# Decoder trunk on one core: start addresses of matmul operands in SBUF, and the place of the column sums in the half steps

## Chip, core and metric

The kernel runs on one core of one Trainium2 chip. The metric is the device time of one execution in microseconds (us); lower is better. Three runs of the kernel before gave 1283.91, 1286.25 and 1288.17 us. Engines are named as the profile names them: PE is the matmul engine (TensorE), PEld its loads of stationary operands, DVE is VectorE, ACT ScalarE, POOL GpSimd, SP SyncE.

## What is computed

A decoder trunk of two layers on x of 256 rows by 1024 columns, all in float32. Each layer is a half step, a mixer with three attention branches, and a second half step. A half step is the feed-forward block:

```python
D_MODEL, SEQ, DEPTH, D_FF = 1024, 256, 2, 2816

def rms_norm(x, g):
    y = x * lax.rsqrt(jnp.mean(x * x, axis=-1, keepdims=True) + EPS)
    return y * g

def swiglu_ffn(x, g, wi, wo):
    a, b = jnp.split(rms_norm(x, g) @ wi, 2, axis=-1)
    return (jax.nn.silu(a) * b) @ wo

for l in range(DEPTH):
    x = x + 0.5 * swiglu_ffn(x, ffn1_norm[l], ffn1_wi[l], ffn1_wo[l])
    h = rms_norm(x, mix_norm[l])
    ...
    x = x + y @ w_out[l]
    x = x + 0.5 * swiglu_ffn(x, ffn2_norm[l], ffn2_wi[l], ffn2_wo[l])
```

## The kernel before

**Weights.** All weights of a layer lie in HBM as a stream of slabs of 128 rows by up to 1024 columns. SP fetches a slab in pieces of 512 columns into `raw`; ACT rounds a piece to its high half (L524) and DVE subtracts to get the low half (L525). The mixer's own loader does the same in L980 and L982. `next_slab` keeps two slabs ahead of the one in use. A product of two split numbers takes three matmuls: high by high, low by high, high by low.

**Two pools hold split slabs.** `slab_tiles` puts a slab into `whi` and `wlo` (pool `wp`, four buffers each, alive all the time) or, within a half step, into `vhi` and `vlo` (pool `fp`, four buffers each, alive during the half step). In a half step slabs 0 to 3 go to `wp`, and slab 6 too (in the first half step of all, slab 8 in its place); so do the 22 slabs of the last half step's down projection.

**Transposed matmuls.** In a half step and in the output projection of the mixer the slab is the stationary operand (128 columns of it at a time), and the moving operand is the activation, transposed, 256 columns for the two tiles of 128 rows. `chunk_T` (L740 to L742) multiplies `hThi`, `hTlo` with the slabs of the up projections: a first chunk "both" of four slabs, whose accumulators hold one gate and one value block, and then, for each chunk of columns, the slabs of the gate and those of the value. `out_T` (L647 to L649) multiplies the result `gh`, `gl` with the down projection, or, at the end of a mixer, `yT` with the output projection. These are 6192 matmuls of 256 columns. The mixer's other projections are the other way round: the slab moves (up to 512 columns) and `hThi`, `hTlo` are stationary (L577 to L579). In the last half step the down projection is in that form too.

**Row scales.** The norm's row factor is applied behind the product. `out_T` adds up squares of the new x in `sq` (L607, L609, and the last addition L611); `sum_squares` lets PE sum the columns with a vector of ones (L617); DVE and POOL make 1/sqrt from it (L623 to L628); `spread_rn` lets PE turn the factors into rows (L719 to L721). Accumulators that are complete before `rows` exists wait in `pend`, and are evacuated when `spread_rn` runs. A phase has eight steps, two for each slab; `scale_cols` is called behind step 5 and `spread_rn` behind step 3, counted from 0. In the first half step of all, `scale_cols` runs in the first gate phase and `spread_rn` in the first value phase behind it; in the other three half steps both come a phase earlier, in the chunk "both" and in the first gate phase.

**Order.** PE runs in the order of the code (a manual schedule). In the mixer, a `Planner` with a clock for each engine settles the order of PE, DVE and ACT when the program is built. Elsewhere the order on DVE and ACT is settled by the framework's scheduler at build time. Within an engine, work is done strictly in that order.

**Where operands begin.** The pools lay tiles one behind another in each partition, so a tile's size shifts those behind it. In the built program the start addresses, modulo 512 bytes, are:

| operand | role in the transposed matmuls | before | after |
|---|---|---|---|
| `hThi`, `hTlo` | moving | 0 | 192 |
| `gh`, `gl` | moving | 0 | 192 |
| `yT` | moving | 320 | 192 |
| `whi`, `wlo` | stationary | 0 | 0 |
| `vhi` | stationary | 192 | 0 |
| `vlo` | stationary | 448 | 0 |

The 128 columns of a stationary operand are 512 bytes and the 256 columns of a moving one are 1024, so every matmul of a kind has the same remainder. For the mixer's `hThi`, `hTlo` and the last half step's `gh`, `gl`, which are stationary, the remainder is 0 in both kernels.

Of the kernel before, what the change touches and what calls it, by code (L numbers as in the profile page):

```python
# [10 lines left out]
F = mybir.dt.float32  # L11
R = mybir.dt.float32r
# [341 lines left out]
WARM = 9  # L354
TAIL = 3

MIX_SLABS = 69
# [13 lines left out]
def decoder_trunk(ctx, tc, xt_in, wts, lcon, cst, out, depth=DEPTH):  # L371
# [21 lines left out]
    def big_tile(name, dt=F, shape=(128, D)):  # L393
        return hp.tile(list(shape), dt, tag="hy", name=name, bufs=6)
# [102 lines left out]
    def slab_tiles(i):  # L497


        j = stream[i][1] % (len(plan) - FFN_SLABS)  # L500
        end = FFN_SLABS - DFF // 128 if i >= len(stream) - FFN_SLABS else FFN_SLABS
        if not 4 <= j < end or j == 6 and i != j or i == 8:
            return tuple(wp.tile([128, 1024], R, tag=t, name=t) for t in ("whi", "wlo"))
        if own:
            return own.pop()
        return tuple(fpool[0].tile([128, 1024], R, tag=t, name=t, bufs=W_BUFS) for t in ("vhi", "vlo"))
# [79 lines left out]

    def new_T():

        n = NT * D
        return tuple(hp.tile([128, n + p], R, tag=t, name=t)[:, p:].rearrange("p (k t n) -> p k t n", t=NT, n=128)  # L590
                     for t, p in (("hThi", 128), ("hTlo", 0)))

# [44 lines left out]

    def out_T(src, kts, gi, between=None, scale=None):

# [17 lines left out]
        sls = [next_slab() for _ in range(TAIL)]  # L657
        hq, sq = nxt[0] = new_T(), big_tile("sq")
        for b in range(KT // 2):
# [35 lines left out]
    def ffn(l, gi):  # L695
        first = l == 0 and gi == 0
        last = l == depth - 1 and gi == 2
        if first:
            nxt[0] = new_T(), big_tile("sq")
        hq, sq = nxt[0]  # L700
        with ExitStack() as es:
            fp = fpool[0] = es.enter_context(tc.tile_pool(name="fp", bufs=2))
            gq = (fp.tile([128, 96 + DFF * NT], R, name="gh", bufs=1)[:, 96:].rearrange(
                      "p (k t n) -> p k t n", t=NT, n=128),
                  fp.tile([128, DFF * NT + 48], R, name="gl", bufs=1)[:, :DFF * NT].rearrange(
                      "p (k t n) -> p k t n", t=NT, n=128))
            vhi = fp.tile([128, 1024], R, tag="vhi", name="vhi", bufs=W_BUFS)
            rows = fp.tile([128, 320], F, name="rows", bufs=1)[:, 0:S].rearrange("p (t n) -> p t n", t=NT)
            own.append((vhi, fp.tile([128, 1024], R, tag="vlo", name="vlo", bufs=W_BUFS)))
# [3 lines left out]
            def spread_rn():  # L713

                tp = tp_tile()
                b = fp.tile([128, 512], F, tag="gate", name="rnb")
                for t in range(NT):
                    c = slice(t * 128, (t + 1) * 128)
                    nc.vector.tensor_copy(b[:, c], rn[t][:, 0:1].to_broadcast([128, 128]))  # L719
                    nc.tensor.transpose(tp[:, c], b[:, c], ident)  # L720
                nc.scalar.activation(rows.rearrange("p t n -> p (t n)"), tp[:, 0:S], AF.Copy)  # L721
                for f in pend:
                    f()
                del pend[:]
                spread[0] = True

# [19 lines left out]

            spread, gates = [False], {}

            def soon(f, *a):
                if spread[0]:  # L750
                    f(*a)
                else:
                    pend.append(lambda: f(*a))
# [75 lines left out]
            if first:  # L829
                first_steps()  # L830
            else:
                drain(chunk_T(512, both), lambda i: scale_cols() if i == 5 else None)

# [10 lines left out]
            def hook(i):  # L844
                if ci == 0 and first:
                    if i == 5:
                        scale_cols()
                elif ci == 0 and i == 3:
                    spread_rn()
                if last and ci and i == 3:  # L850
                    x_rows(ci - 1)
                hook2(i)

            def first_spread(i):
                if i == 3:
                    spread_rn()
                hook2(i)
# [5 lines left out]
            for ci, (f0, fn) in enumerate(FFN_CHUNKS[1:]):  # L863
# [8 lines left out]
                drain(chunk_T(fn, gate_T), hook)  # L872
                drain(chunk_T(fn, value_at(f0 // 128)), first_spread if first and ci == 0 else hook2)

# [5 lines left out]
            else:  # L880
                def scale(a):
                    u = fp.tile([128, 512], F, tag="g", name="u")
                    by_rows(u, a)
                    return u
                out_T(gq, DFF // 128, 3 * l + gi + 1, between, scale)


    def mixer(l):
# [38 lines left out]
        pl = Planner()  # L927
        spawn = pl.spawn
        ordered = tc.manual_schedule(engines={nc.vector.engine, nc.scalar.engine})
        ordered.__enter__()  # L930
# [111 lines left out]
        def scales():  # L1042

            k = yield "P", 0.4, 0.6, (Tok(7.0),), (s_tp,)
            a = sum_squares(sq)
# [896 lines left out]
        def y_first(t):  # L1942
            k = yield use_t(4, ev_y[0][t], slots=(s_tp,))
            if not yT:
                yT.extend(mp.tile([128, 128 + NT * 1024], R, tag=f"V{i}", name="yT")[:, 80:80 + NT * 1024].rearrange(
                    "p (k t n) -> p k t n", t=NT, n=128) for i in (1, 0))
# [29 lines left out]
        nc.scalar.preload_act_table_set("silu_and_others")  # L1976
        out_T(yT, KT, 3 * l + 2, y_T)
        es.close()
# [40 lines left out]
```

## Time and profile before

| | before |
|---|---|
| median of 3 runs | 1286.25 us |
| profiled execution: its own time | 1286.52 us |
| profiled execution: span from the first to the last instruction | 1284.4 us |
| mean granted TensorE clock | 0.997 |
| DVE busy | 928.2 us (72%) |
| ACT busy | 790.1 us (62%) |
| read from HBM | 254.91 MB, 225 GB/s over the span |

The span is 2.1 us shorter than the time of its execution; times within the kernel below are counted from the span's start. The stages can be told from the first use of their operands on PE: first half step to 192.9 us, mixer to 434.9, its output projection and the second half step to 640.8, first half step of the second layer to 828.9, mixer to 1069.4, and the rest to the end.

Matmuls overlap in their pipeline. The duration of one in the profile (about 280 ns for 256 columns) is longer than the distance from its start to the next one's start, and it is that distance that adds up to the time.

### The profile page before, as it was taken

The page shows a single profiled execution, that of the slowest core. Times are in us where ns is not written, and L with a number is a line of the kernel's source. Part 1 is how long each engine was busy: PE and PEld are TensorE (multiplying, and loading weights), DVE is VectorE, ACT ScalarE, POOL GpSimd, SP SyncE. Part 2 cuts the span into 40 slices and gives each one's busy share as a digit, 9 for nine tenths or more (in the row PEclk, how much of TensorE's full clock was granted, in tenths as well). Part 3 has the DMA queues.
Part 4 walks back from the last instruction along what each step waited for, and adds up shares of the span by engine and source line. Part 5 has one row for each costly group of instructions (what it writes and reads, how often), then busy time and mean ns, then how long its engine had stood idle before and what let it go on. Part 6 is the DMA issues. An engine that isn't in the chain of part 4 may idle for free.

```text
span 1284.4 us, 25746 instructions
## 1 busy us (share of the span) xinstructions
PE 1266.3 (99%) x9215; PEld 1174.9 (91%) x9215; DVE 928.2 (72%) x1924; ACT 790.1 (62%) x1627; POOL 104.7 (8%) x164
## 2 busy tenths in 40 slices
PE   9999999999999999999989999999999999999998
PEld 9999998878877899999989999988888779999987
DVE  7776667978898776776667676779768887765653
ACT  6555557777887465565545565577757774655542
POOL 0012100210000001121000121011100000000000
PEclk9999999999999999999989999999999999999999
DMA  8789985556645567899757899664786455566653
GB/s 282 249 285 330 339 284 175 178 181 212 205 127 169 165 221 240 279 333 332 253 165 266 287 336 349 207 195 149 256 289 218 141 170 166 187 189 183 213 164 115
DMA packets 150959, 291.74 MB, mean 227 GB/s; under 512 B 17840, under 2 KB 19504, under 8 KB 150832
## 3 DMA queue, kind: packets, MB, share of 16 engines
q1 hardware_dynamic: 140976, 258.12, 62.0%
q0 software_dynamic: 9856, 31.99, 6.7%
q8 instruction: 72, 1.18, 0.4%
q14 instruction: 55, 0.45, 0.1%
HBM read 254.91 MB, written 34.60 MB: 225 GB/s over the span
## 4 chain that ended last, share of the span: by engine, by line
PE 85%; DVE 5%; ACT 4%; DMA 2%; issue 2%; POOL 0%; SPq 0%; DVEq 0%; ACTq 0%
PE acc L740 12%; PE acc L742 12%; PE acc L741 12%; PE acc L577 9%; PE acc L579 9%; PE acc L578 9%; PE acc L647 5%; PE acc L648 5%; PE acc L649 5%; DMA raw<-in_wts 2%; PE tp L1545 1%; DVE wlo L982 1%; ACT whi L980 1%; DVE hTlo L599 1%; ACT wf L1504 1%
## 5 line engine op out<-in xcount | busy, mean ns | idle before, releaser
L525 DVE TENSOR_TENSOR vlo<-raw,vhi 128x512 fp32r<-128x512 f32 x444 | 288.0, 687 | 107.0 <-ACT vhi L524 106.4
L524 ACT ACTIVATE vhi<-raw 128x512 fp32r<-128x512 f32 x444 | 258.2, 622 | 156.7 <-PE acc L741 53.5
L740 PE MATMUL acc<-hThi,vhi 128*128 128x256 f32 x1248 | 346.9, 278 | 0.0
L742 PE MATMUL acc<-hThi,vlo 128*128 128x256 f32 x1248 | 346.5, 278 | 0.0
L741 PE MATMUL acc<-hTlo,vhi 128*128 128x256 f32 x1248 | 346.2, 277 | 0.0
L741 PEld LDWEIGHTS acc<-hTlo,vhi 128*128 128x128 f32 x1248 | 234.4, 188 | 0.0
L742 PEld LDWEIGHTS acc<-hThi,vlo 128*128 128x128 f32 x1248 | 234.4, 188 | 0.0
L740 PEld LDWEIGHTS acc<-hThi,vhi 128*128 128x128 f32 x1248 | 234.2, 188 | 0.0
L577 PE MATMUL acc<-whi,hThi 128*128 128x512 f32 (+2 forms) x416 | 163.4, 393 | 0.0
L579 PE MATMUL acc<-whi,hTlo 128*128 128x512 f32 (+2 forms) x416 | 158.6, 381 | 0.0
L578 PE MATMUL acc<-wlo,hThi 128*128 128x512 f32 (+2 forms) x416 | 158.1, 380 | 0.0
L982 DVE TENSOR_TENSOR wlo<-raw,whi 128x512 fp32r<-128x512 f32 x216 | 141.3, 679 | 21.3 <-ACT whi L980 20.1
L980 ACT ACTIVATE whi<-raw 128x512 fp32r<-128x512 f32 x216 | 126.3, 617 | 43.1 <-PE acc L579 23.3
L649 PE MATMUL acc<-gh,vlo 128*128 128x256 f32 x528 | 146.4, 277 | 0.0
L647 PE MATMUL acc<-gh,vhi 128*128 128x256 f32 x528 | 146.3, 277 | 0.0
L648 PE MATMUL acc<-gl,vhi 128*128 128x256 f32 x528 | 146.3, 277 | 0.0
L525 DVE TENSOR_TENSOR wlo<-raw,whi 128x512 fp32r<-128x512 f32 x116 | 75.5, 684 | 44.0 <-ACT whi L524 43.7
L524 ACT ACTIVATE whi<-raw 128x512 fp32r<-128x512 f32 x116 | 68.0, 621 | 58.6 <-PE acc L579 26.4
L544 DVE TENSOR_TENSOR elo<-eraw,ehi 128x512 fp32r<-128x512 f32 x60 | 41.5, 692 | 84.1 <-ACT ehi L543 84.1
L543 ACT ACTIVATE ehi<-eraw 128x512 fp32r<-128x512 f32 x60 | 37.9, 632 | 103.8 <-DMA eraw<-in_wts 100.4
L648 PEld LDWEIGHTS acc<-gl,vhi 128*128 128x128 f32 x528 | 99.2, 188 | 0.0
L649 PEld LDWEIGHTS acc<-gh,vlo 128*128 128x128 f32 x528 | 99.1, 188 | 0.0
(319 smaller groups left out, 2417.4 us busy)
## 6 DMA issues: line engine op xcount, KB each, us to landing
raw<-in_wts SPq DMA_DIRECT2D x764, 256.0 KB, 3.3
eraw<-in_wts SPq DMA_DIRECT2D x60, 256.0 KB, 5.1
early<-ehi POOLq DMA_DIRECT2D x60, 256.0 KB, 4.0
early<-elo POOLq DMA_DIRECT2D x60, 256.0 KB, 4.5
whi<-early SPq DMA_DIRECT2D x60, 256.0 KB, 3.8
wlo<-early SPq DMA_DIRECT2D x60, 256.0 KB, 3.9
xd<-x SPq DMA_DIRECT2D x4, 512.0 KB, 2.7
x<-xd SPq DMA_DIRECT2D x4, 512.0 KB, 3.6
```

The costliest lines, as they stand in the source:

```text
L524: nc.scalar.activation(hi[:, c:c + m], raw[:, :m], AF.Copy)
L525: nc.vector.tensor_tensor(lo[:, c:c + m], raw[:, :m], hi[:, c:c + m], op=OP.subtract)
L577: nc.tensor.matmul(o, a[0], b[0], start=start, stop=False)
L578: nc.tensor.matmul(o, a[0], b[1], start=False, stop=False)
L579: nc.tensor.matmul(o, a[1], b[0], start=False, stop=stop)
L647: nc.tensor.matmul(o, sl[0][:, w], h, start=k == 0 and c == 0, stop=False)
L648: nc.tensor.matmul(o, sl[0][:, w], l_, start=False, stop=False)
L649: nc.tensor.matmul(o, sl[1][:, w], h, start=False, stop=k == kts - 1 and c == 1)
L740: nc.tensor.matmul(o, sl[0][:, w], h, start=k == 0 and c == 0, stop=False)
L741: nc.tensor.matmul(o, sl[0][:, w], l_, start=False, stop=False)
L742: nc.tensor.matmul(o, sl[1][:, w], h, start=False, stop=k == KT - 1 and c == 1)
L982: nc.vector.tensor_tensor(hl[1][:, c:c + m], raw[:, :m], hl[0][:, c:c + m], op=OP.subtract)
```

## The change

All slabs now begin at multiples of 512 bytes, whether in `wp` or in `fp`, and the moving operands of the transposed matmuls begin 192 bytes (`MOVING` = 48 elements) behind such a multiple; `new_T` and `out_T` take that shift as `at`. The exceptions for slabs 6 and 8 go. `scale_cols` and `spread_rn` stand where they stood in the first half step, for all four. In the mixer the planner starts with DVE's clock at 7.0 and ACT's at 3.0, and takes the column sums to be possible at 10.0 in place of 7.0.

```diff
+MOVING = 48
...
-        if not 4 <= j < end or j == 6 and i != j or i == 8:
+        if not 4 <= j < end:
             return tuple(wp.tile([128, 1024], R, tag=t, name=t) for t in ("whi", "wlo"))
...
-    def new_T():
+    def new_T(at):
         n = NT * D
-        return tuple(hp.tile([128, n + p], R, tag=t, name=t)[:, p:].rearrange("p (k t n) -> p k t n", t=NT, n=128)
-                     for t, p in (("hThi", 128), ("hTlo", 0)))
+        return tuple(hp.tile([128, n + 128], R, tag=t, name=t)[:, at:at + n].rearrange("p (k t n) -> p k t n", t=NT, n=128)
+                     for t in ("hThi", "hTlo"))
...
-            nxt[0] = new_T(), big_tile("sq")
+            nxt[0] = new_T(MOVING), big_tile("sq")
...
-            gq = (fp.tile([128, 96 + DFF * NT], R, name="gh", bufs=1)[:, 96:].rearrange(
-                      "p (k t n) -> p k t n", t=NT, n=128),
-                  fp.tile([128, DFF * NT + 48], R, name="gl", bufs=1)[:, :DFF * NT].rearrange(
-                      "p (k t n) -> p k t n", t=NT, n=128))
+            at = 96 if last else MOVING - 32
+            gq = tuple(fp.tile([128, DFF * NT + n], R, name=nm, bufs=1)[:, at:at + DFF * NT].rearrange(
+                "p (k t n) -> p k t n", t=NT, n=128) for nm, n in (("gh", 128), ("gl", 96)))
...
-            rows = fp.tile([128, 320], F, name="rows", bufs=1)[:, 0:S].rearrange("p (t n) -> p t n", t=NT)
+            rows = fp.tile([128, S], F, name="rows", bufs=1).rearrange("p (t n) -> p t n", t=NT)
...
-                drain(chunk_T(512, both), lambda i: scale_cols() if i == 5 else None)
+                drain(chunk_T(512, both))
...
             def hook(i):
-                if ci == 0 and first:
-                    if i == 5:
-                        scale_cols()
-                elif ci == 0 and i == 3:
-                    spread_rn()
+                if ci == 0 and i == 5:
+                    scale_cols()
...
-                drain(chunk_T(fn, value_at(f0 // 128)), first_spread if first and ci == 0 else hook2)
+                drain(chunk_T(fn, value_at(f0 // 128)), spread if ci == 0 else hook2)
...
-                out_T(gq, DFF // 128, 3 * l + gi + 1, between, scale)
+                out_T(gq, DFF // 128, 3 * l + gi + 1, 0 if gi == 0 else MOVING, between, scale)
...
         pl = Planner()
         spawn = pl.spawn
+        pl.clock.update(V=7.0, A=3.0)
...
-            k = yield "P", 0.4, 0.6, (Tok(7.0),), (s_tp,)
+            k = yield "P", 0.4, 0.6, (Tok(10.0),), (s_tp,)
...
-                yT.extend(mp.tile([128, 128 + NT * 1024], R, tag=f"V{i}", name="yT")[:, 80:80 + NT * 1024].rearrange(
+                yT.extend(mp.tile([128, 128 + NT * 1024], R, tag=f"V{i}", name="yT")[:, MOVING:MOVING + NT * 1024].rearrange(
...
-        out_T(yT, KT, 3 * l + 2, y_T)
+        out_T(yT, KT, 3 * l + 2, MOVING, y_T)
```

PE, second half step of the first layer, around the column sums (`att` from `sq`). Before, they stand behind the third slab, `whi_6138`:

```order
L740 MATMUL acc_6137<-hThi_6024,whi_6138 128x256
L741 MATMUL acc_6137<-hTlo_6025,whi_6138 128x256
L742 MATMUL acc_6137<-hThi_6024,wlo_6139 128x256
L617 MATMUL att_6238<-gcol_106,sq_6026 128x1 x2
L740 MATMUL acc_6136<-hThi_6024,whi_6172 128x256
```

Now they stand behind the seventh, `vhi_6274`:

```order
L740 MATMUL acc_6273<-hThi_6024,vhi_6274 128x256
L741 MATMUL acc_6273<-hTlo_6025,vhi_6274 128x256
L742 MATMUL acc_6273<-hThi_6024,vlo_6275 128x256
L618 MATMUL att_6376<-gcol_106,sq_6026 128x1 x2
L740 MATMUL acc_6272<-hThi_6024,vhi_6308 128x256
```

From the half step's start to the sums, PE has 168 matmuls in place of 72, and the same holds in the second layer's two half steps.

DVE at the start of the first mixer, where the squares' last addition (`sq` 128x256) releases the column sums. Before:

```order
L599 SCALAR_TENSOR_TENSOR hTlo_2685<-x_75,gcol_106,hThi_2684 128x256 x2
L609 TENSOR_TENSOR sq_2686<-sq_2686 128x512
L982 TENSOR_TENSOR wlo_2895<-raw_2896,whi_2894 128x512
L611 TENSOR_TENSOR sq_2686<-sq_2686 128x256
L982 TENSOR_TENSOR wlo_2895<-raw_2903,whi_2894 128x512
L623 TENSOR_SCALAR ss_2921<-att_2906 128x2
```

And now:

```order
L600 SCALAR_TENSOR_TENSOR hTlo_2685<-x_75,gcol_106,hThi_2684 128x256 x2
L610 TENSOR_TENSOR sq_2686<-sq_2686 128x512
L980 TENSOR_TENSOR wlo_2898<-raw_2899,whi_2897 128x512
L980 TENSOR_TENSOR wlo_2898<-raw_2906,whi_2897 128x512
L612 TENSOR_TENSOR sq_2686<-sq_2686 128x256
L624 TENSOR_SCALAR ss_2924<-att_2902 128x2
```

The last addition has moved behind one more low half of a slab. On PE the sums stand behind the mixer's first 36 matmuls in both kernels.

DVE in the second half step of the first layer, from the row factors (`rn`) to the first evacuations (`gate`, `g`, `gl`). Before:

```order
L628 TENSOR_SCALAR rn<-rs 128x2 x3
L719 COPY rnb<-rn 128x128 x2
L544 TENSOR_TENSOR elo<-eraw,ehi 128x512
L525 TENSOR_TENSOR vlo<-raw,vhi 128x512 x4
L756 TENSOR_TENSOR gate<-acc,rows 128x512
L769 TENSOR_TENSOR g<-acc,gate 128x512
L756 TENSOR_TENSOR gate<-acc,rows 128x512
```

And now:

```order
L629 TENSOR_SCALAR rn<-rs 128x2 x3
L719 COPY rnb<-rn 128x128 x2
L526 TENSOR_TENSOR vlo<-raw,vhi 128x512 x2
L545 TENSOR_TENSOR elo<-eraw,ehi 128x512
L526 TENSOR_TENSOR vlo<-raw,vhi 128x512 x4
L756 TENSOR_TENSOR gate<-acc,rows 128x512 x2
L769 TENSOR_TENSOR g<-acc,gate 128x512
L526 TENSOR_TENSOR vlo<-raw,vhi 128x512
L756 TENSOR_TENSOR gate<-acc,rows 128x512
```

Four accumulators, not two, now wait for the row factors, and three slabs' low halves, not two, stand between the factors and the first evacuation.

More of the change, by code (lines that the diff above doesn't have):

```diff
@@ L636, in drain, with out_T @@
                 hook(i)
-    def out_T(src, kts, gi, between=None, scale=None):
+    def out_T(src, kts, gi, at, between=None, scale=None):
         accs = [acc_tile() for _ in range(KT // 2)]
@@ L657, in out_T @@
         sls = [next_slab() for _ in range(TAIL)]
-        hq, sq = nxt[0] = new_T(), big_tile("sq")
+        hq, sq = nxt[0] = new_T(at), big_tile("sq")
         for b in range(KT // 2):
@@ L724, in spread_rn @@
                 del pend[:]
-                spread[0] = True
+                spreaded[0] = True
             def chunk_T(n, evac):
@@ L745, in chunk_T @@
                         yield
-            spread, gates = [False], {}
+            spreaded, gates = [False], {}
             def soon(f, *a):
-                if spread[0]:
+                if spreaded[0]:
                     f(*a)
@@ L852, in hook, with spread @@
                 hook2(i)
-            def first_spread(i):
+            def spread(i):
                 if i == 3:
```

## The prediction

> **What bounds the kernel now.** I read the page's head and its chain first, then PE's windows stage by stage, then what PE waited for.
>
> ```profile
> span 1284.4 us, 25746 instructions
> PE 1266.3 (99%) x9215; PEld 1174.9 (91%) x9215; DVE 928.2 (72%) x1924; ACT 790.1 (62%) x1627; POOL 104.7 (8%) x164
> ...
> PE 85%; DVE 5%; ACT 4%; DMA 2%; issue 2%; POOL 0%; SPq 0%; DVEq 0%; ACTq 0%
> ```
>
> PE is busy 99% of the span and carries 85% of the chain that ended last. So a change pays only if it takes away one of PE's few waits, or if a matmul takes less time from its start to the next one's. The second is not in a duration: it is a window's length over the number of matmuls in it.
>
> ```profile
> core 0: us, PE busy (x), PEclk, DMA share, GB/s
> 17.20:25.30 8.10, 8.10 (x74) 1.00 0.79 252
> 25.70:192.80 167.10, 167.10 (x1420) 1.00 0.87 298
> 438.10:458.30 20.20, 20.20 (x174) 1.00 0.50 156
> 471.80:640.80 169.00, 169.00 (x1492) 1.00 0.86 289
> 641.00:649.30 8.30, 8.30 (x71) 1.00 0.12 36
> 654.20:659.60 5.40, 5.40 (x26) 0.50 0.75 278
> 668.40:828.80 160.40, 160.40 (x1418) 1.00 0.86 292
> 1072.60:1092.80 20.20, 20.20 (x174) 1.00 0.48 155
> 1106.30:1133.80 27.50, 27.50 (x243) 1.00 0.54 172
> 1134.20:1220.30 86.10, 86.10 (x735) 1.00 0.64 195
> ```
>
> All are windows of the same matmul, 256 columns of float32, with PE never idle. The count holds the two or three that had begun before the window, so I take 2.4 off. 668.4 to 828.8 gives 160.4 / 1415.6 = 113.3 ns; 25.7 to 192.8 gives 167.1 / 1417.6 = 117.9; 641.0 to 649.3 gives 8.3 / 69 = 120. Three paces, then, at the same granted clock. I call them A (113.3), B (117.8) and C (120.0). The mean duration of a group tells them apart as well:
>
> ```profile
> L740 PE MATMUL acc<-hThi,vhi 128*128 128x256 f32 x296 | 81.7, 276 | 0.0
> L740 PE MATMUL acc<-hThi,vhi 128*128 128x256 f32 x257 | 71.7, 279 | 0.0
> L740 PE MATMUL acc<-hThi,whi x24: 283/283/283, 640.8 to 649.1; 128*128 128x256 f32 x24
> L647 PE MATMUL acc<-yT,whi x48: 279/279/363, 441.3 to 458.0; 128*128 128x256 f32 x48
> ```
>
> 276 ns is A (480 to 640 us), 279 B (40 to 180), 283 C. C belongs to `whi`, the one stationary operand that begins, modulo 512 bytes, where its moving operand does. A and B share their addresses (`hThi` at 0, `vhi` at 192, `vlo` at 448), so between these two it isn't the address alone. What turns A into B is a break in the stream:
>
> ```profile
> 25.02 0.28 PE L740 MATMUL acc<-hThi,vhi 128*128 128x256 f32 x1
> ...
> 25.36 0.50 PE L617 MATMUL att<-gcol,sq 128*128 128x1 f32 x4
> 25.72 0.36 PE L740 MATMUL acc<-hThi,vhi 128*128 128x256 f32 x1
> ...
> 26.16 0.28 PE L740 MATMUL acc<-hThi,vhi 128*128 128x256 f32 x1
> ...
> 26.52 0.28 PE L740 MATMUL acc<-hThi,vhi 128*128 128x256 f32 x1
> ```
>
> Three matmuls take 0.34 us before the column sums (25.02 to 25.36) and 0.36 behind them, and it stays so for 167 us. Between the last two windows above stand the transposes of `x_rows` at 1133.8 us, and the pace changes there too (27.5 us for 243, 86.1 for 735). The way back to A leads, wherever the trace shows it, through a slab in `whi` at pace C:
>
> ```profile
> L740 PE MATMUL acc<-hThi,vhi 128*128 128x256 f32 x8 | 2.2, 279 | 0.0
> L740 PE MATMUL acc<-hThi,whi 128*128 128x256 f32 x7 | 2.0, 283 | 0.0
> L740 PE MATMUL acc<-hThi,vhi 128*128 128x256 f32 x7 | 1.9, 276 | 0.0
> ```
>
> These are three windows one behind another, 662.6 to 665.1, 665.8 to 668.2 and 668.7 to 671.0 us: B before slab 6, C in it, A behind it, until 828.8.
>
> **The change part by part.** The profiled execution took 1286.52 us, 0.3 above the median, so what I take off it is taken off the median too.
>
> *Column sums a phase later.*
>
> ```profile
> 649.33 0.28 PE L742 MATMUL acc<-hThi,wlo 128*128 128x256 f32 x1
> 653.29 0.99 PE L617 MATMUL att<-gcol,sq 128*128 128x1 f32 x4 [3.68 <-DVE sq L611]
> ...
> PE att L617 <- DVE sq L611: 8.9, 5, 3.7
> PE att L617 <- DVE sq L611: 1.1, 1, 1.1
> PE att L617 <- DVE sq L611: 1.7, 1, 1.7
> ```
>
> PE waits five times for DVE's last addition of squares, 8.9 us in all; the last two rows are the two mixers' (windows at 190 and 830 us). The three half steps hold 8.9 - 1.1 - 1.7 = 6.1 us. In the largest, `sq` is ready for PE at 653.3, 12.5 us behind the first matmul at 640.8. With 168 matmuls ahead of them the sums come 168 x 0.1133 = 19.0 us behind it: 6.5 us of room, so the wait goes. With it goes the half clock behind it (0.50 from 654.2 to 659.6): 5.4 us for some 25 matmuls that take 25 x 0.1133 = 2.8, and the sums' own 0.85 us (653.29 to 654.14) against 0.36 in the first half step, 0.5. Together 6.1 + 2.6 + 0.5 = 9.2 us.
>
> What is late next? The first half step already runs the new order: its window from 25.7 to 192.8 is busy for 167.10 of 167.10 us, with `spread_rn` and four held accumulators in it. The other three add two `ehi`/`elo` pieces in that stretch. DVE works off three low halves of two pieces (0.68 us each, by the row of the next part) and one `elo` before the first evacuation, 7 x 0.68 = 4.8 us if none is done ahead, and PE needs the next accumulator 48 matmuls or 5.4 us behind the row factors' transposes. That is cover of 0.6 us; I take nothing, and 1 us for each of three at worst.
>
> *Mixer.* There the sums keep their place on PE, and the last addition moves behind one more low half:
>
> ```profile
> 200.12 0.68 DVE L982 TENSOR_TENSOR wlo<-raw,whi 128x512 fp32r<-128x512 f32 x1
> 200.72 0.42 DVE L611 TENSOR_TENSOR sq<-sq 128x256 f32<-128x256 f32 x1
> ```
>
> PE waits for it already, so each mixer loses the 0.60 us from start to start: +1.2. The planner's other moves swap groups of matmuls without adding any; the two waits there, 1.1 + 1.7 us, bound them either way: -2.8 (both gone) to +2.8.
>
> *Addresses.* No matmul is added. B fills 167.1 + 20.2 + 20.2 + 86.1 = 293.6 us of the windows above. At A they would take 113.3 / 117.8 of that: -11.2. C is run by the 480 matmuls with `whi` against `hThi`, less some 80 at other paces: 400 x 6.7 ns = 2.7. So if everything ran at A, -13.9. If everything ran at B, A's windows (8.1 + 169.0 + 160.4 + 27.5 = 365 us) grow by 117.8 / 113.3: +14.5, and C's 400 save 2.2 ns each: -0.9. If everything ran at C: 365 x 0.0591 + 293.6 x 0.0187 = +27.1. Moving at 192 against stationary at 0 occurs nowhere in the trace; `yT` at 320 against 0 is the nearest row, and it ran at B (279 ns) from breaks on. I still take A. After a break, a distance of zero ends at C and one of 192 or 448 at B, so the distance does choose the pace; and every distance seen, counted stationary less moving, is 0 or 192 modulo 256 (192, 448, and 0 - 320), while the new one, 0 - 192, is 64. It is a new case, and A is the pace at which half of the matmuls with a distance other than zero already run. With no distance of zero left, what made C goes too.
>
> The Trainium skill's page "SBUF — State Buffer", section "Who interferes with whom", gives TensorE separate read ports for the moving operand and for the weight load and says that it never waits on anyone. By that rule start addresses do nothing; here 276 and 283 ns for `vhi` and `whi` speak against it.
>
> The sum: 1286.5 - 9.2 + 1.2 - 13.9 = 1264.6, so **1265 us**. Its own range is 1261 (the mixers' waits gone and their 1.2 too) to 1270 (planner +2.8, held accumulators +3).
>
> **The rivals.** (1) *Every break ends in B, and nothing leads back.* For it: `yT`, `vhi` behind 25.36 and `vhi` behind 1133.8. The change takes out the `whi` slab that led back to A, and each half step has two breaks or more. Then 1286.5 - 9.2 + 1.2 + 14.5 - 0.9 = 1292, slower. It decides as soon as B holds over about 60% of what is A now, since only 9.2 - 1.2 + 0.9 = 8.9 us stand against 14.5. Against it: the distance is one not seen. (2) *Addresses do nothing in sum*, whether because A and B are spread by chance as now or because they don't matter at all: 1286.5 - 9.2 + 1.2 = 1278.5, perhaps 1.5 less for C. For it: the same addresses gave A and B. This is also what the skill's rule gives. (3) *A new wait takes the place of the old one*: the four held accumulators stop PE at the second chunk of columns. The three later half steps then wait some 2 us each, and with paces as now the time is 1278.5 + 6 = 1284.5, no change. Against it: the first half step. (4) *The new distance is as bad as zero*: C everywhere, 1286.5 - 8.0 + 27.1 = 1306.
>
> **How the numbers follow.** A everywhere 0.55; (2) 0.22; (1) 0.15; (3) 0.04; (4) 0.04. A difference of 0.3%, 3.9 us, is about what a measurement of this kernel can tell from none. A and nearly all of (2) are faster, 0.76; (3) and the edge of (2) and (1) are no change, 0.07; the rest of (1), and (4), are slower, 0.17. A alone holds too little, and with (2) it is 0.77 at most, so the range reaches to (1): 1260 to 1294.
>
> **What would show it.** `L740` to `L742` and `L647` to `L649` at 276 ns in all stages, `yT` too: A. 279 in long stretches: (1) or (2), by where they lie. 283: (4). PE's wait for `sq` gone in the half steps, some 4 us left in the mixers, and a clock of 1.00 at 650 us: the first term. A wait of PE on DVE `gate` or `g` some 33 us into a half step: (3). I am wrong if a distance of -192 is no different from one of 192 or 320.

## Result and profile after

| | median | lowest to highest | runs |
|---|---|---|---|
| before, same chip | 1286.07 us | 1283.91 to 1288.17 | 4 |
| after | 1276.88 us | 1273.79 to 1277.69 | 4 |

The ratio is 0.9924, with a 95% interval of 0.9901 to 0.9947: 9.2 us faster, where 21 were forecast. The time lies within the predicted range; the gain is less than half of the predicted one. The profiled execution after took 1273.79 us, the fastest of the four, so the profile shows a gain of 12.7 us, not of 9.2. The readings from profiles below explain the 12.7.

The head and the chain of the page after:

```profile
span 1271.7 us, 25740 instructions
PE 1257.2 (99%) x9215; PEld 1166.3 (92%) x9215; DVE 925.7 (73%) x1923; ACT 788.5 (62%) x1628; POOL 108.0 (8%) x164
...
PE 90%; DVE 4%; ACT 3%; DMA 2%; issue 1%; POOL 0%; ACTq 0%; DVEq 0%
```

PE still bounds it, with 90% of the chain in place of 85%. PE's windows after, all in the 256-column matmuls, except for the last two, which lie in the mixers just behind the column sums (columns: window, its length, PE busy and number of matmuls, granted clock with 1.00 for PE's full clock, DMA share, GB/s):

```profile
25.70:34.00 8.30, 8.30 (x73) 1.00 0.97 332
34.50:186.00 151.50, 151.50 (x1338) 1.00 0.89 307
479.00:640.00 161.00, 161.00 (x1421) 1.00 0.84 285
649.00:658.00 9.00, 9.00 (x81) 1.00 0.75 254
658.60:808.00 149.40, 149.40 (x1319) 1.00 0.86 297
1126.00:1146.00 20.00, 20.00 (x173) 1.00 0.62 178
1148.00:1170.00 22.00, 22.00 (x196) 1.00 0.59 193
197.70:201.00 3.30, 3.30 (x10) 0.53 0.27 90
826.60:831.60 5.00, 5.00 (x15) 0.50 0.36 114
```

Taking 2.4 off each count as before: the three long windows give 113.4 to 113.5 ns, pace A, the first of them where the kernel before ran 117.9. Pace B is left behind the column sums (8.3 / 70.6 = 117.6, some 72 matmuls until the row factors' transposes) and behind two of the four breaks by `x_rows` (20.0 / 170.6 = 117.2; the next stretch, 22.0 / 193.6 = 113.6, is A again). At 650 us the clock is 1.00 now. But the last two rows show what wasn't there before: the clock halves in the mixers.

What PE waited for, and the two column sums of the mixers (start, duration, engine, line, what; in brackets how long PE idled and for whom):

```profile
PE att L618 <- DVE sq L612: 4.4, 2, 2.3
PE tp L1663 <- DMA zc<-wf: 2.5, 2, 1.7
```

```profile
197.01 0.67 PE L618 MATMUL att<-gcol,sq 128*128 128x1 f32 x4 [2.28 <-DVE sq L612]
825.62 0.98 PE L618 MATMUL att<-gcol,sq 128*128 128x1 f32 x4 [2.13 <-DVE sq L612]
```

The half steps' waits for `sq` are gone. The mixers' have grown from 1.06 and 1.69 us to 2.28 and 2.13. The same before: the row of the waits, the two sums, and the clock behind the second:

```profile
PE tp L1665 <- DMA zc<-wf: 1.3, 1, 1.3
```

```profile
201.29 0.58 PE L617 MATMUL att<-gcol,sq 128*128 128x1 f32 x4 [1.06 <-DVE sq L611]
837.90 0.58 PE L617 MATMUL att<-gcol,sq 128*128 128x1 f32 x4 [1.69 <-DVE sq L611]
```

```profile
838.60:843.20 4.60, 4.60 (x23) 1.00 0.53 161
```

Before, 23 matmuls lie in 4.6 us at full clock; after, 15 of the same kind in 5.0 us at half.

**Stage by stage.** Each length is the distance from the first matmul of a stage to the first of the next, in the profiled execution of each kernel, in us. The half steps 2 and 4 are counted with the output projection ahead of them. e1 to e12 are the experiments below.

| kernel | half step 1 | mixer 1 | half step 2 | half step 3 | mixer 2 | half step 4 |
|---|---|---|---|---|---|---|
| before | 187.8 | 242.0 | 206.0 | 188.0 | 240.5 | 215.0 |
| after | 181.9 | 244.9 | 203.4 | 180.5 | 244.4 | 211.2 |
| e1 after again | 181.6 | 248.7 | 203.4 | 187.5 | 240.7 | 211.2 |
| e2 mixer sums later | 181.3 | 240.6 | 203.4 | 180.5 | 238.8 | 211.1 |
| e3 addresses only | 182.3 | 246.9 | 205.3 | 194.2 | 240.1 | 215.4 |
| e4 order only | 187.8 | 246.8 | 204.4 | 187.0 | 241.6 | 213.6 |
| e5 mixer as before | 181.4 | 242.3 | 203.4 | 180.9 | 244.3 | 211.1 |
| e6 moving at 320 | 188.6 | 240.3 | 209.3 | 187.2 | 238.1 | 214.4 |
| e7 moving at 256 | 191.2 | 243.0 | 214.6 | 190.7 | 238.7 | 217.1 |
| e8 best | 182.5 | 239.1 | 203.4 | 180.9 | 237.9 | 209.5 |
| e9 moving at 448 | 182.0 | 238.8 | 203.4 | 180.6 | 237.8 | 209.9 |
| e10 moving at 128 | 189.3 | 238.7 | 212.4 | 188.6 | 237.9 | 215.5 |
| e11 best again | 181.5 | 238.7 | 203.4 | 180.5 | 237.9 | 209.5 |
| e12 other order of `x_rows` | 184.2 | 239.6 | 203.4 | 180.6 | 237.9 | 209.5 |

From before to after the half steps give 5.9 + 2.6 + 7.5 + 3.9 = 19.9 us, where 23.1 were forecast, and the mixers take 2.9 + 3.9 = 6.8 back, where 1.2 were forecast; 0.4 more lies ahead of the first stage. That is the 12.7.

### The profile page after: what moved, and what is told of

It is laid out like the page before. It is cut to its first block, busy times and chain, and to the rows that moved or that the text cites. A ratio compares the mean times of both kernels' runs of the same rounds, so it can differ in the third digit from the quotient of the medians.

```text
span 1271.7 us, 25740 instructions
## 1 busy us (share of the span) xinstructions
PE 1257.2 (99%) x9215; PEld 1166.3 (92%) x9215; DVE 925.7 (73%) x1923; ACT 788.5 (62%) x1628; POOL 108.0 (8%) x164
## 4 chain that ended last, share of the span: by engine, by line
PE 90%; DVE 4%; ACT 3%; DMA 2%; issue 1%; POOL 0%; ACTq 0%; DVEq 0%
PE acc L740 12%; PE acc L741 12%; PE acc L742 12%; PE acc L578 10%; PE acc L580 10%; PE acc L579 10%; PE acc L648 5%; PE acc L649 5%; PE acc L650 5%; DMA raw<-in_wts 1%; PE tp L1543 1%; DVE wlo L980 1%; ACT whi L978 1%; PE att L1895 1%; DMA zc<-wf 1%
## 5 line engine op out<-in xcount | busy, mean ns | idle before, releaser
L740 PE MATMUL acc<-hThi,vhi 128*128 128x256 f32 x1280 | 355.6, 278 | 0.0
L742 PE MATMUL acc<-hThi,vlo 128*128 128x256 f32 x1280 | 354.7, 277 | 0.0
L741 PE MATMUL acc<-hTlo,vhi 128*128 128x256 f32 x1280 | 354.6, 277 | 0.0
L526 DVE TENSOR_TENSOR vlo<-raw,vhi 128x512 fp32r<-128x512 f32 x452 | 292.3, 685 | 83.9 <-ACT vhi L525 81.9
L740 PEld LDWEIGHTS acc<-hThi,vhi 128*128 128x128 f32 x1280 | 241.0, 188 | 0.0
L741 PEld LDWEIGHTS acc<-hTlo,vhi 128*128 128x128 f32 x1280 | 240.7, 188 | 0.0
L742 PEld LDWEIGHTS acc<-hThi,vlo 128*128 128x128 f32 x1280 | 240.3, 188 | 0.1
L980 DVE TENSOR_TENSOR wlo<-raw,whi 128x512 fp32r<-128x512 f32 x216 | 141.2, 679 | 32.0 <-ACT whi L978 30.9
L978 ACT ACTIVATE whi<-raw 128x512 fp32r<-128x512 f32 x216 | 126.1, 616 | 48.9 <-PE acc L580 28.0
L526 DVE TENSOR_TENSOR wlo<-raw,whi 128x512 fp32r<-128x512 f32 x108 | 70.2, 683 | 42.8 <-ACT whi L525 42.5
L648 PEld LDWEIGHTS acc<-gh,vhi 128*128 128x128 f32 x528 | 99.1, 188 | 0.0
```

Of the source, the lines that this page charges most:

```text
L526: nc.vector.tensor_tensor(lo[:, c:c + m], raw[:, :m], hi[:, c:c + m], op=OP.subtract)
L648: nc.tensor.matmul(o, sl[0][:, w], h, start=k == 0 and c == 0, stop=False)
L740: nc.tensor.matmul(o, sl[0][:, w], h, start=k == 0 and c == 0, stop=False)
L741: nc.tensor.matmul(o, sl[0][:, w], l_, start=False, stop=False)
L742: nc.tensor.matmul(o, sl[1][:, w], h, start=False, stop=k == KT - 1 and c == 1)
L980: nc.vector.tensor_tensor(hl[1][:, c:c + m], raw[:, :m], hl[0][:, c:c + m], op=OP.subtract)
```

## Experiments

All kernels compute the whole result. "Before" is the kernel before, run between them on the same chip: 1286.53 us for e1 to e4, 1286.71 for e5 to e8, 1285.05 for e9 to e11, 1284.86 for e12.

**e1. The changed kernel again**, without an edit.

> The changed kernel once more. Its four times were 1273.8 (the profiled one) and 1277.0, 1276.8, 1277.7 us, so some 3 us vary from one execution to the next. Theory 1, the pace varies: which breaks of the matmul stream leave pace B (279 ns, 117.8 from start to start) and which leave A (276 ns, 113.3) is not fixed by the program; a second profile then shows B in other or longer stretches of the half steps, 3 us being some 75 us more of B, with the mixers' lengths as before (244.9 and 244.4 us). Theory 2, the clock varies: the half clock behind the mixers' column sums lasts longer or comes a third time; the second profile then has the same paces and mixers 1 to 3 us longer.

1279.17 us (1278.04 to 1280.47), ratio 0.9939 [0.9924, 0.9954]. Its profile (1280.47 us) differs from the first one in two places. Half step 3 is 7 us longer, and its window shows B:

```profile
660.00:755.00 95.00, 95.00 (x809) 1.00 0.82 277
```

95.0 / 806.6 = 117.8 ns, in a place where the first profile ran 113.5. And mixer 1 is 3.8 us longer and mixer 2 3.7 us shorter. In mixer 1 the wait for `sq` grew from 2.28 to 3.35 us and that for `zc` (a tile that a DMA brings) from 1.75 to 2.83, and the clock fell behind both. In mixer 2 the wait for `sq` shrank from 2.13 to 1.92 us, and the clock fell nowhere:

```profile
197.62 0.58 PE L618 MATMUL att<-gcol,sq 128*128 128x1 f32 x4 [3.35 <-DVE sq L612]
283.57 0.63 PE L1663 MATMUL tp<-ident,zc 128*128 128x128 f32 x4 [2.83 <-DMA zc<-wf]
...
835.78 0.58 PE L618 MATMUL att<-gcol,sq 128*128 128x1 f32 x4 [1.92 <-DVE sq L612]
```

```profile
836.40:840.00 3.60, 3.60 (x18) 1.00 0.31 108
284.50:289.00 4.50, 4.50 (x16) 0.62 0.46 162
```

Behind 1.92 us of idling the clock stays 1.00; behind the 2.83 us for `zc` it falls. So one program runs in several ways, some us apart, and a single profile of it is one of them. In half step 3 the pace changes ahead of both breaks: at 639.7 us, 0.7 us into it, two distances from start to start are 0.30 and 0.22 us, and B begins there. The first profile has no such delay at that place.

**e2. The mixers' column sums behind 54 matmuls in place of 36.**

```diff
-            k = yield "P", 0.4, 0.6, (Tok(10.0),), (s_tp,)
+            k = yield "P", 0.4, 0.6, (Tok(13.5),), (s_tp,)
```

> The changed kernel with the mixer's column sums taken to be possible at 13.5 in the planner in place of 10.0: PE has 54 matmuls ahead of them in place of 36, 11 us in place of 7.2, where the squares are ready 9.5 us behind the mixer's start. Theory: the two waits there (2.3 and 2.1 us) and the half clock behind them (366 ns for matmuls that take 200 to 227, over some 3 and 6 us) are what the change lost in the mixers; both go, the mixers become 3 to 4 us shorter each, and the time is 6 to 7 us below that of the changed kernel, near 1270. Rival: the row factors now come later, and PE waits for the first evacuations in place of the sums; the mixers are as long as with the change (244 to 245 us), no change beyond 1 us.

1267.91 us (1263.23 to 1270.43), ratio 0.9858 [0.9838, 0.9878]: 9 to 11 us below the changed kernel, where 6 to 7 were expected. PE no longer waits for `sq` at all, and the clock behind the sums stays up:

```profile
197.76 0.50 PE L618 MATMUL att<-gcol,sq 128*128 128x1 f32 x4
822.24 0.50 PE L618 MATMUL att<-gcol,sq 128*128 128x1 f32 x4
```

```profile
198.20:203.20 5.00, 5.00 (x23) 1.00 0.69 187
822.90:827.90 5.00, 5.00 (x23) 1.00 0.69 209
```

In its profile (1263.23 us, the fastest of the four) the mixers take 240.6 and 238.8 us, 9.9 less than in the changed kernel's profile and 3.1 less than before. So the mixers' loss hangs on the place of the sums.

**e3. The addresses alone**: `scale_cols`, `spread_rn` and the mixer's planner as before.

```diff
-                drain(chunk_T(512, both))
+                drain(chunk_T(512, both), lambda i: scale_cols() if i == 5 else None)
...
-        pl.clock.update(V=7.0, A=3.0)
...
-            k = yield "P", 0.4, 0.6, (Tok(10.0),), (s_tp,)
+            k = yield "P", 0.4, 0.6, (Tok(7.0),), (s_tp,)
```

> Only the addresses of the change (moving at 192, every slab at 0, no slab 6 or 8 in the other pool); column sums and planner as in the kernel before. Theory, the distance between stationary and moving operand chooses what a break leaves behind: pace A in most of the half steps (276 ns in the first half step behind its row factors, and in the output projections), so -10 to -12 us, with the three waits for the squares (6 us) and the half clock behind the longest still there: 1274 to 1276. Rival, the paces in the changed kernel come from where its breaks stand: paces as in the kernel before (279 ns in the first half step), 1284 to 1288.

1290.62 us (1287.33 to 1297.78), ratio 1.0038 [1.0020, 1.0055]: a miss, it isn't faster than before. The waits for `sq` grew from 8.9 to 11.5 us, since PE arrives at the sums earlier, and half steps 3 and 4 fell to B:

```profile
PE att L618 <- DVE sq L612: 11.5, 5, 4.1
```

```profile
666.00:808.00 142.00, 142.00 (x1208) 1.00 0.88 295
```

142.0 / 1205.6 = 117.8. Mixer 1 is 4.9 us longer than before: its order is that of before, but PE's wait for `sq` grew from 1.06 to 3.00 us, with half clock behind it. Half step 1, where the sums already had the later place, shows the addresses' gain undisturbed: 182.3 us against 187.8.

**e4. The order alone**: the addresses, and the exceptions for slabs 6 and 8, as before.

```diff
-        if not 4 <= j < end:
+        if not 4 <= j < end or j == 6 and i != j or i == 8:
...
-            at = 96 if last else MOVING - 32
+            gq = (fp.tile([128, 96 + DFF * NT], R, name="gh", bufs=1)[:, 96:].rearrange(
...
```

> Only the order of the change (column sums and row factors a phase later, the planner's clocks), with the addresses of the kernel before and its slabs 6 and 8 in the other pool. Theory, at the old distances every break leaves B and only a slab at pace C behind the last break leads back: slab 6 now stands ahead of both breaks, so the half steps run at B to their end (+12 us), against -9 for the waits and +5 to +7 for the mixers: 1292 to 1297. Rival, the addresses do nothing and the order alone made the changed kernel quicker: 1274 to 1278.

1286.16 us (1284.10 to 1288.52), ratio 0.9997 [0.9986, 1.0008]: nothing in sum, neither the gain of 9 us that the lost waits alone would give nor the loss that B behind every break would bring. The old addresses don't leave B behind every break: half step 2 ran at A behind its sums and its row factors (150.0 us for 1323.6 matmuls, 113.3 ns). Half step 3 lost its wait of 3.7 us and the half clock behind it, but ran at B behind the row factors (126.0 / 1069.6 = 117.8), where before slab 6 had led it back to A:

```profile
202.90:206.90 4.00, 4.00 (x14) 0.57 0.37 131
...
674.00:800.00 126.00, 126.00 (x1072) 1.00 0.90 301
```

```profile
202.33 0.58 PE L617 MATMUL att<-gcol,sq 128*128 128x1 f32 x4 [1.82 <-DVE sq L611]
```

The first row, and the sums ahead of it, are mixer 1: half clock here too, with the old addresses. In sum the half steps are 4.1 us shorter than before and the mixers 5.8 longer; this profiled execution (1288.52 us) was the slowest of ten. By the medians the addresses alone give +4.1 us and the order alone -0.4; both in one kernel give -7.4 on the same chip (e1), -9.2 in the first measurement. In these profiles they need one another: the earlier arrival that faster matmuls bring makes the old place of the sums worse, and without the new distance the lost wait is paid back in pace.

**e5. The changed kernel, with the mixer's order as before.**

```diff
-        pl.clock.update(V=7.0, A=3.0)
...
-            k = yield "P", 0.4, 0.6, (Tok(10.0),), (s_tp,)
+            k = yield "P", 0.4, 0.6, (Tok(7.0),), (s_tp,)
```

> The change with the mixer's order as before (no extra low half ahead of the last addition of squares, column sums asked for at 7.0). Theory 1, the mixers' loss comes from the order on DVE (one low half more ahead of the last addition): the two waits for sq fall back to the 1.1 and 1.7 us of before, no half clock, the mixers fall back by some 5 us, about 1271 us. Theory 2, the loss comes from PE arriving earlier, since the down projections ahead of the mixers run at the fast pace now and take 2.35 us less, while the sums are still asked for behind 36 matmuls: the waits are 1.1 + 2.35 = 3.4 and 1.7 + 2.35 = 4.0 us, a stretch at half clock behind each, about 1277 to 1280 us.

1274.25 us (1271.03 to 1275.28), ratio 0.9903 [0.9882, 0.9924], between the two theories. DVE's rows in mixer 1, first after, then e5 (x2 marks two in one row):

```profile
195.25 1.28 DVE L980 TENSOR_TENSOR wlo<-raw,whi 128x512 fp32r<-128x512 f32 x2
196.46 0.41 DVE L612 TENSOR_TENSOR sq<-sq 128x256 f32<-128x256 f32 x1
```

```profile
194.81 0.68 DVE L979 TENSOR_TENSOR wlo<-raw,whi 128x512 fp32r<-128x512 f32 x1
195.41 0.42 DVE L612 TENSOR_TENSOR sq<-sq 128x256 f32<-128x256 f32 x1
```

One low half less stands ahead of the last addition, and the wait in mixer 1 is 1.77 us, against 2.28 after and 1.06 before. But this one profile can't tell the theories apart. Up to these sums PE, DVE and ACT run the same instructions in the same order in e3, and there the wait was 3.00 us:

```profile
198.39 0.77 PE L618 MATMUL att<-gcol,sq 128*128 128x1 f32 x3 [3.00 <-DVE sq L612]
```

So the wait of one and the same order varies by 1.2 us, twice the 0.60 of the low half. All waits for `sq` of the mixers with 36 matmuls ahead of the sums tell more, sorted by the mixer's order and by the pace of the half step ahead (us):

| half step ahead | order of before | order of the change |
|---|---|---|
| B | 1.06 (before), 1.01 (e3) | 1.82 and 1.81 (e4), 1.92 (e1) |
| A | 1.69 (before), 1.77 and 2.12 (e5), 3.00 (e3) | 2.28 and 2.13 (after), 3.35 (e1) |

Behind a half step at B the order of the change costs some 0.8 us. Pace A ahead of the mixer adds from 0.3 to 2 us more. So both theories hold a part of the loss. PE reaches the sums 7.4 to 7.6 us behind the mixer's first matmul in all of these; what varies is DVE, whose last addition ends 8.2 to 10.6 us behind that matmul. The two mixers of e5 also separate the wait from the clock:

```profile
195.98 0.58 PE L618 MATMUL att<-gcol,sq 128*128 128x1 f32 x4 [1.77 <-DVE sq L612]
822.92 0.96 PE L618 MATMUL att<-gcol,sq 128*128 128x1 f32 x4 [2.12 <-DVE sq L612]
```

```profile
196.50:200.00 3.50, 3.50 (x18) 1.00 0.50 135
823.90:828.90 5.00, 5.00 (x14) 0.50 0.46 145
```

1.77 us cost no clock, and mixer 1 takes 242.3, 1.7 more than in e2: about the wait itself. 2.12 us cost 5 us at half clock, and mixer 2 takes 244.3, 5.5 more than in e2. So a wait of some 2 us costs about its own length, or about 3 us more.

**e6 and e7. The moving operands at 320 and at 256 bytes**, on e2.

```diff
-MOVING = 48
+MOVING = 80
```

(64 in e7.)

> The kernel with the mixers' sums later, but moving operands 320 bytes beyond a multiple of 512 in place of 192; so the distance from moving to stationary is 192 again, as vhi had it against hThi. Theory distance chooses the pace: the old kind of distance leaves B behind half of the breaks or more, half steps 6 to 12 us longer than with 192, 1274 to 1282 us, and groups of L740 at 279 ns in stretches of more than a thousand matmuls. Rival, any distance that isn't zero does the same and only chance tells runs apart: 1264 to 1271 us, A behind nearly all row factors' transposes.

> As the last one, but moving operands at 256 bytes: distance 256, zero modulo 256. If the distance counts modulo 256, this is what whi had against hThi: pace C (283 ns, 120 ns from start to start) everywhere, up to 6192 x 6.7 ns = 41 us on top of 1268, about 1305 us. If it counts modulo 512: A or B as with other distances, 1264 to 1282 us, no group at 283 ns.

e6: 1286.21 us (1280.19 to 1288.02), ratio 0.9988 [0.9969, 1.0008]. e7: 1302.08 us (1301.30 to 1302.86), ratio 1.0123 [1.0096, 1.0151]. Against e2 that is 18 and 34 us for nothing but where the operands begin. e6 lies above the 1274 to 1282 that were expected, e7 at the 1305 of its first theory. The same stretch of half step 1, e6 first, then e7:

```profile
36.00:193.00 157.00, 157.00 (x1336) 1.00 0.88 295
```

```profile
36.00:195.00 159.00, 159.00 (x1327) 1.00 0.86 288
```

157.0 / 1333.6 = 117.7 is B, and it holds behind 17 of the 18 breaks that can be told; 159.0 / 1324.6 = 120.0 is C, and it holds nearly everywhere. The sums' waits are gone in both, as in e2. So with everything else the same the distance decides how often each pace comes, and 256 counts as zero. It doesn't decide alone: the kernel before and e4 have e6's distance modulo 256, and ran long stretches at A (1415.6 matmuls from 668.4 us on in the prediction's windows, half step 2 in e4).

**e8. A better kernel**: e2, with `zc` planned to land 5.5 us behind its issue, and the breaks by `x_rows` in pairs a step apart.

```diff
-            z = Tok(k2.t + 3.0)
+            z = Tok(k2.t + 5.5)
...
-                if last and ci and i == 3:
-                    x_rows(ci - 1)
+                if last and ci in (1, 3) and i in (3, 4):
+                    x_rows(ci - 1 + i - 3)
```

> The kernel with the mixers' sums later, and two edits: the planner takes zc to land 5.5 us behind its issue in place of 3.0 (PE waited 2.2 us for it in the two mixers), and the four breaks by x_rows come in two pairs a step apart, so that the slow pace behind the first of a pair lasts 12 matmuls in place of 400 or so. Theory: waits for zc gone (-2.2), B behind x_rows nearly gone (-1.6): about 1264 us. Rival: the wait for zc moves to what is planned behind it, and a second break doesn't lead back to A: 1268 us, or up to 3 us more.

1260.15 us (1259.02 to 1263.16), ratio 0.9801 [0.9776, 0.9826]. PE no longer waits for `zc`; the mixers are 2.5 us shorter than in e2, and half step 4 is 1.6 shorter. By the ratios e8 is 7 us below e2; the two profiled executions (1263.23 and 1260.80 us) show 2.4 of it.

**e9 and e10. The moving operands at 448 and at 128 bytes**, on e8.

> The best kernel so far (sums later, zc later, x_rows in pairs; 1260.2 us), with the moving operands 448 bytes beyond a multiple of 512 in place of 192. Theory, the distance from stationary to moving counts modulo 256: 448 is 192 there, so the same paces at the same places, A behind the row factors' transposes, 1257 to 1264 us. Rival, it counts modulo 512: a new case, and as 320 and 256 gave 10 to 35 us more, about 1275 us.

> As the last one, at 128 bytes, which hasn't been seen. Distances so far: 0 and 256 gave C, 320 gave B, 192 gave A behind two breaks in three. If pace worsens the nearer the distance comes to a multiple of 256, 128 is the farthest and gives A at least as often as 192: 1257 to 1261 us, and A behind the column sums and x_rows too. If 192 is a place of its own: B behind most breaks, as at 320, 1272 to 1280 us.

e9: 1262.95 us (1259.85 to 1266.06), ratio 0.9821 [0.9780, 0.9862]. e10: 1289.94 us (1289.62 to 1290.38), ratio 1.0032 [1.0017, 1.0047]. Half step 1 in e9, then in e10:

```profile
35.00:186.00 151.00, 151.00 (x1334) 1.00 0.88 308
```

```profile
36.00:194.00 158.00, 158.00 (x1334) 1.00 0.87 292
```

151.0 / 1331.6 = 113.4: 448 runs like 192, so the count is modulo 256. 158.0 / 1331.6 = 118.7 at 128: neither B nor C but short stretches of both in turn, from the first matmul to the last. Both theories that were written down for 128 (A, or B) are wrong.

**e11. The best kernel again.**

> The best kernel so far once more, in more rounds: 1260 us, 1257 to 1264, ratio to before 0.978 to 0.982; stages as in its first profile where the paces behind breaks are as they were, up to 4 us more where one half step falls to B.

1259.76 us (1258.99 to 1263.15), ratio 0.9807 [0.9782, 0.9833]: by the ratios 15 us below the changed kernel. The waits that PE has left in it, and the stretch between the two pairs of `x_rows`:

```profile
PE acc L421 <- DVE gcol L445: 1.5, 1, 1.5
PE tp L1543 <- ACT wf L1534: 1.1, 3, 0.6
PE acc L578 <- DVE hvl L1006: 0.5, 1, 0.5
```

```profile
1111.80:1153.80 42.00, 42.00 (x373) 1.00 0.62 189
```

42.0 / 370.6 = 113.3 ns.

**e12. The pairs of `x_rows` in another order**, on e8: units 0 and 2, then 1 and 3.

```diff
-                    x_rows(ci - 1 + i - 3)
+                    x_rows((ci - 1) // 2 + 2 * (i - 3))
```

> The best kernel, with the x_rows breaks in another order: the first pair now transposes the first half of the columns of both row tiles (units 0 and 2), the second pair the second half (1 and 3). In five profiles so far units 0 and 2 left B and units 1 and 3 left A, in whatever pace the stream was before. Theory 1, which operand the break reads decides (units 0 and 2 read one x buffer, 1 and 3 another): B for all 372 matmuls behind the first pair, no B at the second, 1.6 us more in the last half step: about 1261 to 1262 us where the rest is as in the best profile. Theory 2, the count decides (two transpose buffers taken in turn, or every second break): B for 12 and A behind both pairs as now, 1260 us.

1262.54 us (1262.23 to 1262.86), ratio 0.9822 [0.9794, 0.9851]. Behind the first pair:

```profile
1115.00:1156.00 41.00, 41.00 (x364) 1.00 0.59 188
```

41.0 / 361.6 = 113.4: A, though unit 2, which had left B in every run with 192 so far, is now the last before it. What `x` buffer the break reads doesn't matter; it is the second break that leaves A, whatever it reads. (The 2.7 us over e11 in half step 1 are no matter of pace: the down projection runs at A there, but PE waits five times for DVE and ACT, 2.2 us in all, where e11 has no such wait.) Whether it counts because every second break does, or because the two transpose buffers in PSUM are taken in turn, wasn't separated.

## Where the prediction was right and where it failed

**The half steps' waits** (-9.2): right. No wait for `sq` is left in a half step, and the clock at 650 us is 1.00. As a gain of its own it isn't there, though: in e4 only 4.1 of the 9.2 are left in the half steps, as the pace behind the row factors fell, and the mixers take them back.

**Four held accumulators** (nothing, 3 us at worst): right. No row of PE's waits after names `gate` or `g`; rival (3) didn't happen.

**Addresses** (-13.9, all at A): the choice of A was right, the size too large. In the profiled run B is left for some 135 matmuls at the start, 4 x 72 behind the sums, 2 x 195 behind `x_rows` and some 70 of `yT`: about 880 x 4.5 ns = 4.0 us that A everywhere had counted as won. Together with the row above, 23.1 were forecast and 19.9 came. And e1 shows a run of the same program with half step 3 at B, 7 us longer. The reason given, that 0 - 192 is a new case modulo 256, holds: e6 with the old remainder goes to B nearly everywhere, e9 with the new one and another remainder modulo 512 to A. Rival (1), every break ends in B and nothing leads back, is what e6 shows at the old distance, 1286 us; its premise that the `whi` slab led back to A held in three half steps before, and is no longer needed at 192. In the first half step it didn't hold: slab 8 ran at C from about 28.6 to 31.5 us, and the stretches on both sides of it at B. Rival (2), addresses do nothing, would have come closest in the number (1278.5), for another reason: in e2, e6, e7, e9 and e10 they are worth up to 34 us.

By the section "Who interferes with whom" of the Trainium skill's page "SBUF — State Buffer", TensorE waits on no one; start addresses would do nothing then. Five distances gave 113.4, 113.4, 117.7, 118.7 and 120.0 ns for the same matmuls: the measurement decides against it.

**The mixers** (+1.2): this is the step that failed. It counted one more low half ahead of the last addition, 0.60 us in each, and bounded the planner's other moves by the two waits there. It was +6.8 us. From the rows above:

- The waits for `sq` grew by 1.22 + 0.44 = 1.7 us, close to the 1.2. By the table under e5 the order is worth some 0.8 us, and pace A in the half step ahead 0.3 to 2 us more. PE's earlier arrival at the mixer was in the prediction's own terms (a down projection at A) and wasn't carried over to the next wait.
- Behind both waits the clock now falls, which was left out altogether. From the start of the sums to the start of the 25th matmul behind them, 5.68 and 5.69 us became 7.26 and 8.72: 4.6 us. This is the largest part. The half step at 650 us, with 3.68 us of idling and 0.50 behind it, stood in the prediction as a gain; that the mixers' waits of 1.1 and 1.7 us were just short of the same fate wasn't asked.
- The waits for `zc` grew from 1.3 to 2.5 us: 1.2.

These make 7.5; the 0.7 that the mixers gained elsewhere weren't traced. e2 is the test: without the waits for `sq` the same change gives 1267.9 us. The forecast had 1261 for that case, and with the 4.0 us of B that it left out 1265.

The mixers' 5.6 us above the forecast, the half steps' 3.2 below it and the 0.4 ahead of the first stage make the 9.2 us by which the profiled gain (12.7) fell short of the 21.9 that the sum gave for the same profile. The other 3.5 us, between the fastest execution and the median, have no profile of their own; e1's profile (B in half step 3, longer waits in mixer 1) shows what kind of difference they can be.

Two things stay open: what decides between A and B behind a break at a given distance (the second of two breaks leaves A in e8, e9, e11 and e12; behind row factors it was A nearly always with 192 or 448, but not in half step 3 of e1 and e3 and half step 4 of e3 and e9), and why DVE ends the last addition up to 1.4 us later in one run than in another with the same order (e3 against e5).

## What to carry to other kernels

A wait of PE has two prices: its length, and the half clock that may follow it; a stage that gets faster runs into the next wait sooner, so ask of each short wait behind it what it grows to. Here falls were seen behind waits from 1.7 us on (e3, half step 4) and never behind shorter ones. If PE is always busy, look at the distance from start to start of equal matmuls, not at their durations or at busy shares, and try a few start addresses of the moving operand against the stationary one: at 192 modulo 256 bytes the kernel of e2 is 18 to 34 us faster than at 64 or 0. Take several profiles of one program before reading a difference of a few us.

## What the runs showed of the hardware

- The time of a 256-column float32 matmul behind another depends on where the moving operand begins against the stationary one, modulo 256 bytes, all at a granted clock of 1.00. 0 gives 120.0 ns and 128 gives 118.7 as a mixture; 192 gives 113.4 (117.6 to 117.8 in stretches behind some breaks); 64 gave 117.7 nearly everywhere in e6, but both 113.3 and 117.8 in long stretches of the kernel before.
- Idle stretches of PE that halve the clock aren't told by their length: 1.70 us (e3, half step 4), 1.82 (e4), 2.12, 2.13 and 2.28 did, 1.75 (after, `zc`), 1.77 (e5) and 1.92 (e1) did not. The Trainium skill's page "TensorE: Matmul & The Clock Gate", section "What's actually happening", tells of a window of some 3.4 us that runs freely, and of a fall behind a window that is idle. The traces agree with the window: in the profile after, the granted clock falls at 197.36 and 825.42 us and comes back at 200.78 and 832.24, which is 1, 183 and 2 times 3.413 us from one to the next, and in every trace all changes lie on such a grid. That a whole window must be idle does not fit.

What the place in the grid does can be read from the traces. These are windows of the grid, in e4 around the wait of 1.82 us, and in e1 around that of 1.92:

```profile
199.62:203.03 3.41, 1.58 (x10) 1.00 0.63 203
203.03:206.45 3.42, 3.42 (x11) 0.50 0.26 90
834.36:837.77 3.41, 1.99 (x12) 1.00 0.60 185
837.78:841.19 3.41, 3.41 (x17) 1.00 0.33 115
```

The 1.82 us lie in one window with the sums; the 1.92 are cut by a border, and 0.51 of them belong to the window ahead. Counting the sums as idle too, since they move one column each, all fourteen traces fall into two groups: ahead of the kernel's last matmuls, each of the 13 windows at full clock with 1.93 us or more of idling was followed by half clock, and none with 1.85 or less was. The half clock then lasted one window, or two where most of the sums' time fell into the first of them; that is the 1.6 and the 3.0 us of the two mixers after. Where the grid lies differs between executions of one program: modulo 3.413 us its borders are 2.80 us behind the span's start in the profile after, 1.51 in e1. The spread of e4's ten executions fits that: the three with a mean clock of 1.000 took 1284.1 to 1284.7 us, the three with 0.994 or 0.995 took 1286.5 to 1288.5. This count was made from the traces afterwards, with ends of matmuls that the profile models, and no run was made to test it.
